# Attention in steps of two query blocks, with an order on TensorE that the scheduler may not change

## The chip, the cores and the metric

The kernel runs on one core of one Trainium2 chip. What counts is the device time of one execution of the whole program in microseconds (us). The time of the kernel before is the median of three runs.

## The reference

One layer of a hybrid decoder, for 2048 tokens of width 1024, in float32. After a projection, four mixers work on slices of its columns: stick-breaking attention (4 heads), a gating MLP over chunks, the RWKV-7 recurrence (4 heads), and forgetting attention (4 heads). Their outputs are joined and projected, and a mixture of experts follows. The change touches the two kinds of attention:

```python
HEAD_DIM, SEQ, BLOCK_Q = 64, 2048, 128
def stick_breaking_attention(q, k, v):          # 4 heads, "SB"
    for q0 in range(0, seq, BLOCK_Q):
        z = einsum('bhqd,bhkd->bhqk', q[q0:k_end], k[:k_end]) * scale
        log_one_minus = where(strict, log_sigmoid(-z), 0.0)
        between = cumsum(log_one_minus, axis=3, reverse=True) - log_one_minus
        attn = where(strict, exp(log_sigmoid(z) + between), 0.0)
        outs.append(einsum('bhqk,bhkd->bhqd', attn, v[:k_end]))
def forgetting_attention(q, k, v, log_f):       # 4 heads, "FX"
    cum = cumsum(log_f, axis=2)
    for q0 in range(0, seq, BLOCK_Q):
        logits = einsum('bhqd,bhkd->bhqk', q[q0:k_end], k[:k_end]) * scale
        logits = logits + cum[q0:k_end, None] - cum[None, :k_end]
        probs = softmax(where(causal, logits, -inf), axis=-1)
        outs.append(einsum('bhqk,bhkd->bhqd', probs, v[:k_end]))
```

Stick-breaking needs no softmax: the products of (1 - sigmoid) run along the keys from the newest to the oldest, which the kernel does with one scan per row of queries.

## The kernel before

The program is traced in this order: norm and input projection, RWKV-7 (lines 600 to 960, its products on TensorE are small), attention (from line 312), output projection (L1033 to L1106), experts. A scheduler in the compiler then orders the instructions of each engine by a simulated time line, so that RWKV-7 and attention, which do not depend on each other, lie interleaved on all engines.

Attention goes head by head, the four SB heads first and then the four FX heads. A head has 8 blocks `b` of 256 queries (two row blocks `i = 2b, 2b+1` of 128 queries, one for each half `a`), and its keys lie in chunks `c` of 512. One pass over one chunk for both halves is called a step here; a head has 20 steps. A step is made of these parts:

- logits: for each half, two float32r products (high and low part of the keys, L375 and L376) into one PSUM bank of a pool of four ("bk"), and on the diagonal a mask product (L378).
- SB: tanh on ScalarE (L390), a scale and shift on GpSimd (L391), the scan on VectorE (L393) that turns a row of 512 numbers into stick weights `S`.
- FX: VectorE adds the gates and takes the running row maximum (L402). After the last chunk of a half, two small VectorE operations make the bias (L408, L409), ScalarE takes the exponentials of all its chunks (L413), and small VectorE operations make the reciprocal of the sum (L415, L416).
- `weigh`: for each pair `p` of 128-key tiles (two pairs in a chunk), four transposes of `S` through TensorE into one bank "bk" (L425, three on the diagonal), one copy to SBUF on ScalarE (L427, tile `tq`), and two products with the values (L431; in fp32 the trace shows two records for each) into the accumulator `o`, which has one PSUM bank.
- `out`: after the last pair, VectorE and ScalarE add the halves of `o` (L442 to L457; for FX two more transposes bring the reciprocal, L455), and SP stores to `mixT`.

The transposes of one step are traced in turn with the logits of later ones by generators, half by half and pair by pair, and the scheduler may then move all of them. TensorE (PE), ScalarE (ACT), VectorE (DVE) and GpSimd (POOL) each take their instructions in the order that the scheduler wrote.

After attention the output projection reads `mixT` back in blocks of 128 tokens and multiplies it by `w_out` (L1103 to L1105).

Of the kernel before, what the change touches and what calls it, by code (L numbers as in the profile page):

```python
# [8 lines left out]
F32 = mybir.dt.float32  # L9
# [3 lines left out]
AF = mybir.ActivationFunctionType  # L13
# [294 lines left out]
def attention(tc, K, ctx, sT, sV, cumD, mixT):  # L308
# [17 lines left out]
    class Head:  # L326
# [54 lines left out]
        def spans(self, i):  # L381
            n = (i + 1) * 128
            return [(c, c * 512, min(512, n - c * 512)) for c in range(i // 4 + 1)]
# [12 lines left out]
        def softmax(self, i, S, rq):  # L396
            mx = None
            for c, x0, w in self.spans(i):
                z = self.logits(i, c, w)
                S[c] = sp.tile([128, 512], F32, name="S", tag="S")  # L400
                m = tp.tile([128, 1], F32, name="m")
                nc.vector.tensor_tensor_reduce(S[c][:, :w], z, self.nk[c][:, :w], 0.125,  # L402
                                               -3.0e38 if mx is None else mx, op0=OP.add, op1=OP.max, accum_out=m)
                mx = m
                yield
            c1 = cq[:, i, self.h:self.h + 1]
            bias = tp.tile([128, 1], F32, name="bias")
            nc.vector.tensor_add(bias, mx, c1)  # L408
            nc.vector.tensor_sub(bias, c1, bias)  # L409
            sm = tp.tile([128, 4], F32, name="sm")  # L410
            n = i // 4 + 1
            for c, x0, w in self.spans(i):
                nc.scalar.activation(S[c][:, :w], S[c][:, :w], AF.Exp, bias=bias, accum_out=sm[:, c:c + 1])  # L413
            if n > 1:
                nc.vector.tensor_reduce(sm[:, 0:1], sm[:, 0:n], AX.X, OP.add)  # L415
            nc.vector.reciprocal(rq, sm[:, 0:1])  # L416

        def weigh(self, b, p, S, o, first, last):
# [7 lines left out]
            tq = tp.tile([128, 512], F32, name="tq")  # L426
            nc.scalar.activation(tq[:, :w], t[:, :w], AF.Copy)  # L427
            for e in range(2):
# [32 lines left out]
        def block(self, b):  # L461
            S = [{}, {}]
            rq = None if self.sb else tp.tile([128, 2], F32, name="rq")
            o = []

            def weigh(p, first, last):
                if first:
                    o.append(po.tile([128, 256], F32, name="o"))
                self.weigh(b, p, S, o[0], first, last)
                if last:  # L470
                    self.out(b, o[0], rq)

            def front(c):
                if b % 2 == 0 and c == b // 2:
                    self.load(c)
                for a in range(2):
                    S[a][c] = sp.tile([128, 512], F32, name="S", tag="S")
                    self.sticks(2 * b + a, c, S[a])
                    yield

            def back(c):
                for p in range(min(2 * c + 1, b), 2 * c - 1, -1):
                    weigh(p, p == b, p == 0)
                    yield

            def front0():
                if b % 2 == 0:
                    self.load(b // 2)
                yield from self.softmax(2 * b, S[0], rq[:, 0:1])

            def mid():
                yield from self.softmax(2 * b + 1, S[1], rq[:, 1:2])

            def back0():
                for p in range(b + 1):
                    weigh(p, p == 0, p == b)
                    yield

            if self.sb:
                return [([front(c)], [], back(c)) for c in range(b // 2, -1, -1)]  # L500
            return [([front0()], [mid()], back0())]

    prev = iter(())
    for sb in (True, False):
        for h in range(NH):
            H = Head(h, sb)
            for b in range(8):
                for first, second, back in H.block(b):
                    for g in first:
                        yield from g  # L510
                    for g in second:
                        for _ in prev:
# [1363 lines left out]
```

## Time and profile before

| | |
|---|---|
| runs of the kernel before | 2602.68, 2606.71, 2612.62 us, median 2606.71 |
| profiled execution | span 2606.8 us from its first to its last instruction, at the median of the runs |
| granted TensorE clock, mean | 0.967 of full speed |
| attention on PE | 615.8 (first L375) to 1520.8 us (last product L431), SB until 1059.5 |
| RWKV-7 on PE | 534 to 1525.5 us |
| output projection on PE | from 1526.3 us |

All times are counted from the start of the span. "Busy" is the time in which an engine executes; an idle stretch of an engine is put down to what ended it, so "PE L425 <- DVE S L393" means that a transpose on PE waited for a scan on VectorE. Matmuls are pipelined in PE, so a record's duration is longer than its distance to the next record's start; it is the distance between starts that adds up. The clock of PE has two levels, 1.2 and 2.4 GHz, shown as 0.5 and 1.0, or as their mean over a stretch.

### The profile page before, as it was taken

How to read it: one execution, taken by the hardware profiler on the slowest of the kernel's cores; microseconds unless marked ns; L12 is line 12 of the kernel's file. 1: busy time of each engine (PE TensorE's matmuls, PEld its weight loads, DVE VectorE, ACT ScalarE, POOL GpSimd, SP SyncE). 2: the span in 40 equal slices, each digit the busy share in tenths (PEclk: the TensorE clock that was granted, in tenths of full speed). 3: DMA queues.
4: the chain of work that ended last, by engine and by line, in shares of the span. 5: the costliest groups of instructions: out<-in, count | busy, mean ns of one | idle time of the engine just before them, and what ended most of it. 6: DMA issues, size and time to landing. Idle time of an engine off the chain costs nothing. (4 is left out here: it accounts for less than half of the span.)

```text
span 2606.8 us, 42226 instructions
## 1 busy us (share of the span) xinstructions
PE 2442.3 (94%) x14802; PEld 1754.4 (67%) x14803; DVE 1675.3 (64%) x3881; ACT 1324.1 (51%) x2527; POOL 675.1 (26%) x691
## 2 busy tenths in 40 slices
PE   7999999997989898999999998997999999999994
PEld 6789998874656564656556667774666666676663
DVE  5313402247797869687685756665677787787885
ACT  5201222224655565675565642223667677776774
POOL 2000000015464647331332022112212232222224
PEclk9999999998989999999999999998999999999997
DMA  8510222125120211111111059443989899899995
GB/s 245 174 59 30 77 69 69 63 67 118 34 60 26 48 41 39 46 55 41 49 32 43 11 187 275 130 122 111 337 271 331 306 329 368 308 321 358 327 317 164
DMA packets 241826, 394.73 MB, mean 151 GB/s; under 512 B 65921, under 2 KB 106753, under 8 KB 241608
## 3 DMA queue, kind: packets, MB, share of 16 engines
q1 hardware_dynamic: 222472, 336.68, 39.1%
q0 software_dynamic: 19136, 55.30, 7.5%
q8 instruction: 118, 1.93, 0.3%
q14 instruction: 100, 0.82, 0.1%
HBM read 319.24 MB, written 76.85 MB: 152 GB/s over the span
## 5 line engine op out<-in xcount | busy, mean ns | idle before, releaser
L72 DVE TENSOR_TENSOR wl<-wr,wh 128x1024 fp32r<-128x1024 f32 x366 | 442.6, 1223 | 114.5 <-ACT wh L71 107.6
L71 ACT ACTIVATE wh<-wr 128x1024 fp32r<-128x1024 f32 x366 | 381.6, 1057 | 138.0 <-PE pg L1446 53.8
L393 DVE TENSOR_TENSOR_SCAN S<-S,zero 128x512 f32<-128x512 f32 (+3 forms) x160 | 197.8, 1246 | 50.5 <-POOL S L391 50.3
L152 PE MATMUL p<-hhi,wh 128*128 128x512 f32 x512 | 206.1, 404 | 14.8 <-ACT hhi L112 6.9
L425 PE MATMUL bk<-ident,S 128*128 128x128 f32 x1088 | 186.3, 292 | 24.5 <-DVE S L393 18.5
L427 ACT ACTIVATE tq<-bk 128x512 f32<-128x512 f32 (+1 forms) x288 | 156.6, 571 | 101.0 <-PE bk L425 81.4
L154 PE MATMUL p<-hhi,wl 128*128 128x512 f32 x512 | 205.2, 401 | 0.0
L153 PE MATMUL p<-hlo,wh 128*128 128x512 f32 x512 | 204.9, 400 | 0.0
L431 PE MATMUL o<-tq,v 128*64 128x256 f32 (+1 forms) x1152 | 189.3, 400 | 4.3 <-ACT tq L427 2.8
L425 PEld LDWEIGHTS bk<-ident,S 128*128 128x128 f32 x1088 | 124.0, 145 | 98.3 <-issue 53.4
L156 DVE TENSOR_TENSOR e<-p,rb 128x512 f32<-128x512 f32 x64 | 43.6, 689 | 198.3 <-PE p L154 183.9
L391 POOL TENSOR_SCALAR S<-S 128x512 f32<-128x512 f32 (+3 forms) x160 | 127.9, 808 | 145.8 <-ACT S L390 129.8
L735 POOL TENSOR_TENSOR k<-big,k 128x512 f32<-128x512 f32 x8 | 14.2, 1774 | 554.8 <-DVE big L734 548.8
L375 PE MATMUL bk<-kh,qs 128*128 128x512 f32 (+2 forms) x320 | 147.7, 462 | 7.2 <-POOL qs L351 4.8
L171 PE MATMUL p<-wh,hhi 128*128 128x256 f32 (+1 forms) x512 | 144.6, 282 | 0.0
L172 PE MATMUL p<-wl,hhi 128*128 128x256 f32 (+1 forms) x512 | 144.3, 282 | 0.0
L173 PE MATMUL p<-wh,hlo 128*128 128x256 f32 (+1 forms) x512 | 143.7, 281 | 0.0
L152 PEld LDWEIGHTS p<-hhi,wh 128*128 128x128 f32 x512 | 97.9, 191 | 40.2 <-ACT hhi L112 6.5
L413 ACT ACTIVATE S<-S,bias 128x512 f32<-128x512 f32 (+3 forms) x160 | 103.6, 649 | 34.2 <-DVE bias L409 33.7
L376 PE MATMUL bk<-kl,qs 128*128 128x512 f32 (+2 forms) x320 | 120.9, 379 | 0.0
L71 ACT ACTIVATE wh<-raw 128x512 fp32r<-128x512 f32 (+1 forms) x52 | 27.6, 589 | 179.2 <-PE p L153 171.7
L1443 PE MATMUL pg<-wh,xh 128*128 128x512 f32 x248 | 102.6, 414 | 12.6 <-ACT s L1450 12.6
(559 smaller groups left out, 6144.6 us busy)
## 6 DMA issues: line engine op xcount, KB each, us to landing
wr<-in SPq DMA_DIRECT2D x386, 512.0 KB
raw<-in SPq DMA_DIRECT2D x108, 256.0 KB
sT<-e SPq DMA_DIRECT2D x64, 256.0 KB
raw<-sT SPq DMA_DIRECT2D x128, 128.0 KB
mr<-mixT SPq DMA_DIRECT2D x16, 512.0 KB
xt<-in SPq DMA_DIRECT2D x16, 512.0 KB
xacc<-xt SPq DMA_DIRECT2D x16, 512.0 KB
h2D<-h SPq DMA_DIRECT2D x16, 512.0 KB
```

The source lines that it names most:

```text
L71: nc.scalar.activation(hi, raw, AF.Copy)
L72: nc.vector.tensor_sub(lo, raw, hi.bitcast(F32))
L152: nc.tensor.matmul(p, wh[:, k, ms], hi[j][:, k], start=(k == 0), stop=False)
L153: nc.tensor.matmul(p, wh[:, k, ms], lo[j][:, k], start=False, stop=False)
L154: nc.tensor.matmul(p, wl[:, k, ms], hi[j][:, k], start=False, stop=(k == KD - 1))
L171: nc.tensor.matmul(p, a, wh[:, k], start=first and k == 0, stop=False, skip_group_check=True)
L172: nc.tensor.matmul(p, a, wl[:, k], start=False, stop=False, skip_group_check=True)
L375: nc.tensor.matmul(z[:, :w], q, self.kh[c][:, :w], start=True, stop=False)
L393: nc.vector.tensor_tensor_scan(r, r, K.zero.to_broadcast([128, w]), 1.0 if c == i // 4 else S[c + 1][:, 0:1], op0=OP.mult, op1=OP.add)
L425: nc.tensor.transpose(t[:, x:x + 128], S[a][j // 4][:, (j % 4) * 128:(j % 4) * 128 + 128], K.ident)
L427: nc.scalar.activation(tq[:, :w], t[:, :w], AF.Copy)
L431: nc.tensor.matmul(o[64 * e:64 * e + 64, o0:256], self.v[j // 4][:, j % 4], tq[:, x0:x1], start=first, stop=last, skip_group_check=True)
```

## The change

In the new code a step is a function `front(c)` that issues the logits of both halves one after the other, and then the tanh and scan, or the maximum, of both. For FX one call of `softmax` after the last chunk serves both halves, with its small VectorE operations on two columns instead of one, and the exponentials of all chunks of both halves in a row, chunk by chunk. `back(ps)` issues the transposes of both pairs of a chunk (`turn`: up to eight, and two copies), and after them all products of both pairs (`weigh`). A `back` is issued after the `front` of a later step (`LAG = 2`, one `back` after each `front`). `tq`, `m` and `rq` have four buffers. All of it stands in `tc.manual_schedule(engines={PE})`, so that attention's instructions keep this order among themselves on PE; the scheduler still puts RWKV-7's between them, and it still orders the other engines.

```diff
-        def sticks(self, i, c, S):
-            x0 = c * 512
-            w = min(512, (i + 1) * 128 - x0)
-            z = self.logits(i, c, w)
+        def sticks(self, i, c, z, S):
+            w = z.shape[-1]
             s = S[c][:, :w]
...
-        def softmax(self, i, S, rq):
-            mx = None
-            for c, x0, w in self.spans(i):
-                z = self.logits(i, c, w)
...
-                yield
-            c1 = cq[:, i, self.h:self.h + 1]
-            bias = tp.tile([128, 1], F32, name="bias")
+        def softmax(self, b, S, mx, rq):
+            c1 = cq[:, 2 * b:2 * b + 2, self.h]
+            bias = tp.tile([128, 2], F32, name="bias")
             nc.vector.tensor_add(bias, mx, c1)
             nc.vector.tensor_sub(bias, c1, bias)
-            sm = tp.tile([128, 4], F32, name="sm")
-            n = i // 4 + 1
-            for c, x0, w in self.spans(i):
-                nc.scalar.activation(S[c][:, :w], S[c][:, :w], AF.Exp, bias=bias, accum_out=sm[:, c:c + 1])
+            sm = tp.tile([128, 2, 4], F32, name="sm")
+            n = b // 2 + 1
+            for c in range(n):
+                for a in range(2):
+                    s = S[a][c][:, 0:min(512, (2 * b + a + 1) * 128 - c * 512)]
+                    nc.scalar.activation(s, s, AF.Exp, bias=bias[:, a:a + 1], accum_out=sm[:, a, c:c + 1])
...
-        def weigh(self, b, p, S, o, first, last):
+        def turn(self, b, p, S):
             t = bank()
...
-            tq = tp.tile([128, 512], F32, name="tq")
+            tq = tp.tile([128, 512], F32, name="tq", bufs=4)
             nc.scalar.activation(tq[:, :w], t[:, :w], AF.Copy)
+            return tq
+
+        def weigh(self, b, p, tq, o, first, last):
...
+            order = [[p for p in range(min(2 * c + 1, b), 2 * c - 1, -1)] for c in chunks]
+            ends = (order[0][0], order[-1][-1])
+            def front(c):
+                if b % 2 == 0 and c == chunks[0]:
+                    self.load(top)
+                z = []
+                for a in range(2):
+                    i = 2 * b + a
+                    S[a][c] = sp.tile([128, 512], F32, name="S", tag="S")
+                    z.append(self.logits(i, c, min(512, (i + 1) * 128 - c * 512)))
+                m = None if self.sb else tp.tile([128, 2], F32, name="m", bufs=4)
+                for a in range(2):
+                    if self.sb:
+                        self.sticks(2 * b + a, c, z[a], S[a])
+                    else:
+                        self.scores(c, z[a], S[a], None if mx[0] is None else mx[0][a], m[:, a:a + 1])
+                mx[0] = None if m is None else [m[:, a:a + 1] for a in range(2)]
+                if not self.sb and c == top:
+                    self.softmax(b, S, m, rq)
+            def back(ps):
+                if ends[0] in ps:
+                    o.append(po.tile([128, 256], F32, name="o"))
+                t = [self.turn(b, p, S) for p in ps]
+                for p, tq in zip(ps, t):
+                    self.weigh(b, p, tq, o[0], p == ends[0], p == ends[1])
+                if ends[1] in ps:
+                    self.out(b, o[0], rq)
...
-    prev = iter(())
-    for sb in (True, False):
...
-                        yield from g
-                    yield from prev
-                    prev = back
-    yield from prev
+            backs = [lambda ps=ps: back(ps) for ps in order]
+            for k, c in enumerate(chunks):
+                yield (lambda: front(c)), ([backs[k]] if self.sb else backs if c == top else [])
+    LAG = 2
+    ready = []
+    n = 0
+    with tc.manual_schedule(engines={mybir.EngineType.PE}):
+        for sb in (True, False):
+            for h in range(NH):
+                H = Head(h, sb)
+                for b in range(8):
+                    for front, backs in H.block(b):
+                        front()
+                        yield
+                        ready += [(n, f) for f in backs]
+                        if ready and ready[0][0] <= n - LAG:
+                            ready.pop(0)[1]()
                             yield
-                            next(prev, None)
-                            next(g, None)
-                        yield from g
+                        n += 1
+        for _, f in ready:
+            f()
+            yield
```

How the order on the engines changes is seen at three places. The first is PE in the first SB head. L375 and L376 are logits, L425 transposes, L431 products; the other lines, here L896 to L917, are RWKV-7's. Before:

```order
L425 MATMUL bk_9957<-ident_68,S_9902 128x128
L375 MATMUL bk_9967<-kh_9564,qs_9791 128x512
L376 MATMUL bk_9967<-kl_9565,qs_9791 128x512
L896 MATMUL bk_5207<-btok_4823,wz_5193 64x64 x4
L915 MATMUL bk_5227<-wz_5193,btok_4823 64x64
L916 MATMUL bk_5227<-kv_4824 64x64
L375 MATMUL bk_9974<-kh_9564,qs_9791 128x512
L376 MATMUL bk_9974<-kl_9565,qs_9791 128x512
L913 MATMUL bk_5206<-qt_5220,M0_5204 64x128 x2
L425 MATMUL bk_9980<-ident_68,S_9934 128x128
```

The same place after, where L420 are transposes and L430 products:

```order
L430 MATMUL o_9869<-tq_9931,v_9576 64x256 x2
L896 MATMUL bk_5207<-btok_4823,wz_5193 64x64 x4
L915 MATMUL bk_5227<-wz_5193,btok_4823 64x64
L916 MATMUL bk_5227<-kv_4824 64x64
L430 MATMUL o_9869<-tq_9938,v_9576 64x256 x2
L375 MATMUL bk_9951<-kh_9566,qs_9775 128x512
L376 MATMUL bk_9951<-kl_9567,qs_9775 128x512
L375 MATMUL bk_9955<-kh_9566,qs_9775 128x512
L376 MATMUL bk_9955<-kl_9567,qs_9775 128x512
L420 MATMUL bk_9965<-ident_68,S_9878 128x128
L420 MATMUL bk_9965<-ident_68,S_9883 128x128 x2
```

The logits of the two halves stood apart, with RWKV-7's instructions and transposes between them; they now stand together, and what RWKV-7 has is put elsewhere, here between the products of a step.

The second place is PE in the last FX head, from the last logits of block 6 (`bk_15628`) to the transposes of that block's own scores (`S_15526`). After the change:

```order
L376 MATMUL bk_15628<-kl_15378,qs_15384 128x512
L378 LDWEIGHTS identb_71
L378 MATMUL bk_15628<-fx_mask_77,identb_71 128x128
...
L420 MATMUL bk_15657<-ident_68,S_15453 128x128
L430 MATMUL o_15574<-tq_15655,v_15144 64x256 x2
L430 MATMUL o_15574<-tq_15662,v_15144 64x256 x2
L420 MATMUL bk_15668<-ident_68,S_15479 128x128
L420 MATMUL bk_15668<-ident_68,S_15484 128x128 x2
L430 MATMUL o_15574<-tq_15672,v_15387 64x256
L430 MATMUL o_15574<-tq_15672,v_15387 64x128
L454 MATMUL bk_15679<-ident_68,rq_15373 128x128 x2
L420 MATMUL bk_15686<-ident_68,S_15526 128x128
```

Where "..." stands are the first seven of eight transposes. No instruction of RWKV-7 is left in this head: on PE the last of them stands ahead of it. The head has only its own products between one step's copies and the next. In the same head before, from the second half's logits of a block of the same size, the transposes of the block before stand between RWKV-7's rows:

```order
L376 MATMUL bk_15799<-kl_15633,qs_15639 128x384
L378 LDWEIGHTS identb_71
L378 MATMUL bk_15799<-fx_mask_77,identb_71 128x128
L425 MATMUL bk_15817<-ident_68,S_15650 128x128
L864 MATMUL bk_9382<-x641_4732,blk_9133 64x64 x4
L883 MATMUL bk_9389<-rhs_9016,xtf0_4716 128x128 x4
L425 MATMUL bk_15826<-ident_68,S_15650 128x128
L375 MATMUL bk_15835<-kh_15062,qs_15639 128x512
L376 MATMUL bk_15835<-kl_15063,qs_15639 128x512
L425 MATMUL bk_15817<-ident_68,S_15704 128x128
```

Each transpose, product and block of logits had others beside it that wait for other things; after, the order is step by step.

The third place is ScalarE at that same spot of the last head: L405 are the exponentials of block 6, L422 the copies behind the transposes. After the change:

```order
L422 ACTIVATE tq_15655<-bk_15650 128x512
L422 ACTIVATE tq_15662<-bk_15657 128x512
L405 ACTIVATE S_15526,sm_15638<-S_15526,bias_15635 128x512
L405 ACTIVATE S_15530,sm_15638<-S_15530,bias_15635 128x512
L405 ACTIVATE S_15563,sm_15638<-S_15563,bias_15635 128x512
L405 ACTIVATE S_15567,sm_15638<-S_15567,bias_15635 128x512
L405 ACTIVATE S_15593,sm_15638<-S_15593,bias_15635 128x512
L405 ACTIVATE S_15597,sm_15638<-S_15597,bias_15635 128x512
L405 ACTIVATE S_15622,sm_15638<-S_15622,bias_15635 128x384
L405 ACTIVATE S_15627,sm_15638<-S_15627,bias_15635 128x512
L422 ACTIVATE tq_15672<-bk_15668 128x384
```

Before (L413 exponentials, L427 copies, L866 and L885 RWKV-7's):

```order
L413 ACTIVATE S_15704,sm_15773<-S_15704,bias_15770 128x512
L413 ACTIVATE S_15728,sm_15773<-S_15728,bias_15770 128x512
L413 ACTIVATE S_15760,sm_15773<-S_15760,bias_15770 128x512
L866 ACTIVATE y6_9387<-bk_9382 64x256
L413 ACTIVATE S_15767,sm_15773<-S_15767,bias_15770 128x256
L885 ACTIVATE wz_9394<-bk_9389 128x512
L413 ACTIVATE S_15784,sm_15809<-S_15784,bias_15806 128x512
L413 ACTIVATE S_15790,sm_15809<-S_15790,bias_15806 128x512
L413 ACTIVATE S_15796,sm_15809<-S_15796,bias_15806 128x512
L413 ACTIVATE S_15803,sm_15809<-S_15803,bias_15806 128x384
L427 ACTIVATE tq_15822<-bk_15817 128x512
```

The exponentials of the two halves were two groups of four that each waited for their own bias; they are one group of eight, and the copy `tq_15672`, for which a product of the block before waits, stands behind all eight.

## Rows read from the trace of the kernel before

**Rows 1.** The page: busy time, share of the span, instructions.

```profile
PE 2442.3 (94%) x14802; PEld 1754.4 (67%) x14803; DVE 1675.3 (64%) x3881; ACT 1324.1 (51%) x2527; POOL 675.1 (26%) x691
```

**Rows 2.** Busy time by stretch: SB, FX, fourth SB head, last FX head.

```profile
core 0: us, PE busy (x) PEld busy (x) DVE busy (x) ACT busy (x) POOL busy (x), PEclk, DMA share, GB/s
615.80:1059.50 443.70, 402.74 (x2904) 253.31 (x2904) 364.92 (x598) 262.47 (x619) 255.32 (x258) 0.93 0.21 53
1059.50:1526.30 466.80, 452.15 (x3471) 286.85 (x3469) 320.58 (x1109) 288.46 (x775) 109.85 (x115) 0.99 0.15 43
953.00:1059.50 106.50, 95.31 (x705) 57.79 (x703) 98.36 (x165) 64.23 (x155) 73.93 (x72) 0.97 0.18 47
1390.70:1520.50 129.80, 128.98 (x995) 83.50 (x993) 73.44 (x268) 78.66 (x208) 11.06 (x15) 0.96 0.10 26
```

**Rows 3.** PE's waits in the SB stretch: total us, times, longest us.

```profile
PE bk L425 <- DVE S L393: 18.5, 22, 2.6
PE bk L845 <- DVE yv L839: 5.6, 6, 1.5
```

**Rows 4.** PE's waits in the FX stretch: total us, times, longest us.

```profile
PE bk L425 <- DVE m L402: 2.9, 5, 1.4
```

**Rows 5.** VectorE's waits in the SB stretch.

```profile
DVE S L393 <- POOL S L391: 50.3, 41, 4.6
```

**Rows 6.** PE's waits for copies, from 600 to 1520 us.

```profile
PE o L431 <- ACT tq L427: 2.8, 7, 0.7
PE bk L425 <- ACT tq L427: 2.1, 3, 1.4
```

**Rows 7.** PE's time line near the end: start us, duration us, instructions.

```profile
1513.32 1.08 PE L431 MATMUL o<-tq,v 128*64 128x256 f32 x8
1514.34 1.09 PE L425 MATMUL bk<-ident,S 128*128 128x128 f32 x8
1515.36 0.65 PE L431 MATMUL o<-tq,v 128*64 128x256 f32 x4
1515.94 0.66 PE L425 MATMUL bk<-ident,S 128*128 128x128 f32 x4
1516.53 0.65 PE L431 MATMUL o<-tq,v 128*64 128x256 f32 x4
```

**Rows 8.** PE's time line where logits end, at two places.

```profile
715.06 0.39 PE L376 MATMUL bk<-kl,qs 128*128 128x512 f32 x1
715.29 0.27 PE L832 MATMUL bk<-ident,xc 128*128 128x128 f32 x1
...
1418.44 0.40 PE L376 MATMUL bk<-kl,qs 128*128 128x512 f32 x1
1418.76 0.65 PE L431 MATMUL o<-tq,v 128*64 128x256 f32 x4
```

**Rows 9.** PE's time line where products wait directly behind their transposes.

```profile
723.81 0.55 PE L425 MATMUL bk<-ident,S 128*128 128x128 f32 x3 [1.73 <-DVE S L393]
725.03 0.65 PE L431 MATMUL o<-tq,v 128*64 128x256 f32 x4 [0.67 <-ACT tq L427]
```

**Rows 10.** ScalarE's time line: exponentials, then two copies.

```profile
1345.40 0.72 ACT L413 ACTIVATE S<-S,bias 128x512 f32<-128x512 f32 x1 [1.16 <-DVE bias L409]
...
1346.12 0.71 ACT L413 ACTIVATE S<-S,bias 128x512 f32<-128x512 f32 x1
...
1347.67 1.09 ACT L427 ACTIVATE tq<-bk 128x512 f32<-128x512 f32 x2 [0.26 <-PE bk L425]
```

**Rows 11.** PE's time line where attention ends and the output projection begins.

```profile
1519.32 1.51 PE L431 MATMUL o<-tq,v 128*64 128x256 f32 x12
1524.13 0.70 PE L688 MATMUL bk<-ident,big 128*128 128x128 f32 x4 [3.30 <-DVE big L684]
...
1526.28 0.77 PE L1103 MATMUL p<-wh,mh 128*128 128x512 f32 x1
...
1529.42 0.50 PE L1103 MATMUL p<-wh,mh 128*128 128x512 f32 x1 [1.17 <-DVE y L938]
```

More of the change, by code (lines that the diff above doesn't have):

```diff
@@ L394, in sticks, with scores @@
                                          1.0 if c == i // 4 else S[c + 1][:, 0:1], op0=OP.mult, op1=OP.add)
-        def softmax(self, i, S, rq):
-            mx = None
-            for c, x0, w in self.spans(i):
-                z = self.logits(i, c, w)
[L400 to L404, printed above, removed]
-                yield
-            c1 = cq[:, i, self.h:self.h + 1]
-            bias = tp.tile([128, 1], F32, name="bias")
+        def scores(self, c, z, S, mx, m):
+            w = z.shape[-1]
+            nc.vector.tensor_tensor_reduce(S[c][:, :w], z, self.nk[c][:, :w], 0.125,
+                                           -3.0e38 if mx is None else mx, op0=OP.add, op1=OP.max, accum_out=m)
+        def softmax(self, b, S, mx, rq):
+            c1 = cq[:, 2 * b:2 * b + 2, self.h]
+            bias = tp.tile([128, 2], F32, name="bias")
             nc.vector.tensor_add(bias, mx, c1)
             nc.vector.tensor_sub(bias, c1, bias)
-            sm = tp.tile([128, 4], F32, name="sm")
-            n = i // 4 + 1
-            for c, x0, w in self.spans(i):
-                nc.scalar.activation(S[c][:, :w], S[c][:, :w], AF.Exp, bias=bias, accum_out=sm[:, c:c + 1])
-            if n > 1:
-                nc.vector.tensor_reduce(sm[:, 0:1], sm[:, 0:n], AX.X, OP.add)
-            nc.vector.reciprocal(rq, sm[:, 0:1])
-        def weigh(self, b, p, S, o, first, last):
+            sm = tp.tile([128, 2, 4], F32, name="sm")
[4 more added lines that the diff above has]
+                    nc.scalar.activation(s, s, AF.Exp, bias=bias[:, a:a + 1], accum_out=sm[:, a, c:c + 1])
+            if n > 1:
+                st = tp.tile([128, 2], F32, name="st")
+                nc.vector.tensor_reduce(st, sm[:, :, 0:n], AX.X, OP.add)
+                nc.vector.reciprocal(rq, st)
+            else:
+                nc.vector.reciprocal(rq, sm[:, :, 0])
+        def turn(self, b, p, S):
             t = bank()
@@ L462, in block @@
             S = [{}, {}]
-            rq = None if self.sb else tp.tile([128, 2], F32, name="rq")
+            rq = None if self.sb else tp.tile([128, 2], F32, name="rq", bufs=4)
+            mx = [None]
             o = []
-            def weigh(p, first, last):
-                if first:
+            top = b // 2
+            chunks = range(top, -1, -1) if self.sb else range(top + 1)
+            order = [[p for p in range(min(2 * c + 1, b), 2 * c - 1, -1)] for c in chunks]
+            ends = (order[0][0], order[-1][-1])
@@ new lines, in front @@
+            def front(c):
[10 more added lines that the diff above has]
+                        self.sticks(2 * b + a, c, z[a], S[a])
+                    else:
+                        self.scores(c, z[a], S[a], None if mx[0] is None else mx[0][a], m[:, a:a + 1])
+                mx[0] = None if m is None else [m[:, a:a + 1] for a in range(2)]
+                if not self.sb and c == top:
+                    self.softmax(b, S, m, rq)
@@ L468, in weigh @@
+            def back(ps):
+                if ends[0] in ps:
                     o.append(po.tile([128, 256], F32, name="o"))
-                self.weigh(b, p, S, o[0], first, last)
-                if last:
+                t = [self.turn(b, p, S) for p in ps]
+                for p, tq in zip(ps, t):
+                    self.weigh(b, p, tq, o[0], p == ends[0], p == ends[1])
+                if ends[1] in ps:
                     self.out(b, o[0], rq)
[L473 to L497, printed above, removed]
```

14 lines of the change are left out of this document (1 added, 13 removed).

## The prediction

> **What bounds the kernel now.** I read the page first: TensorE (PE) is busy 94% of the span, VectorE 64%, ScalarE 51% [rows 1]. An average over stages says little, so I cut attention's stretch into the SB part and the FX part [rows 2]. In FX, PE is busy 452 of 467 us: the time there is PE's work and only 15 us are gaps. In SB, PE is busy 403 of 444 us, at a granted clock of 0.93 (the lower level, 1.2 GHz, for about an eighth of the stretch), and VectorE has 365 us: PE leads, VectorE is near, and in the fourth SB head it is at 98 of 106.5 us, more than PE's 95. The waits say what the gaps of PE are: in SB transposes that wait for a scan, 18.5 us in 22 pieces [rows 3], behind which VectorE itself waits 50 us for GpSimd [rows 5]; in FX almost nothing, 2.9 us for maxima [rows 4]. Waits for copies come to 2.8 + 2.1 us in all of attention [rows 6]. So there are three places for a gain: the amount of PE work, the SB scan waits, and the end of the stage; and one for a loss: the copies, hidden so far.
>
> **The change part by part.** The sum is made against the profiled span, 2606.8 us; the median of the runs is 2606.7, so nothing has to be added.
>
> *Fewer changes of kind on PE.* In the orders, attention's stretch has 1139 runs of one kind of instruction before and 822 after: 280 runs of transposes become 202, 257 of products 203, 266 of logits 168. What does a longer run save? [rows 7] give distances from start to start: eight transposes take 1515.36 - 1514.34 = 1.02 us, four 1516.53 - 1515.94 = 0.59, so one merge saves 2 x 0.59 - 1.02 = 0.16; the products of two tiles (8 records) take 1.02, of one 0.58, a merge saves 0.14. A logits product that is followed by a product with values takes 0.32, by another full-width matmul 0.23 [rows 8], so 0.09 is saved. That makes 78 x 0.16 + 54 x 0.14 + 98 x 0.09 = 12.5 + 7.6 + 8.8 = 29 us. Pricing every neighbouring pair of the two orders by the median start distance that such a pair has in the trace gives 21 to 25. I take **-25**, bounds 0 and -29.
>
> The rows show switching as a real cost, 1.16 to 1.18 us for two single runs where one long run takes 1.02 [rows 7]. The Trainium skill, TensorE: Matmul & The Clock Gate, section "Step-by-step: what each phase is for", says that the next tile's weights are loaded while the current matmul runs, pulled ahead of it, which would make a change of kind free; by that rule this term would be nothing and the sum 2626. The trace does not agree with it at these places.
>
> *Scan waits.* The distance from an SB logits product to the first transpose of the same scores, counted in PE work of the orders without any wait, has a median of 6.6 us before and 8.7 after; the shortest twentieth is below 4.4 before and below 6.8 after. Two whole steps now lie between, so most of the 18.5 us should go. What it exposes: if VectorE is late as a whole, the lag does not help. I keep 3 us of it: **-15**, bounds 0 and -18.5. FX's 2.9 us for maxima lies in the same place and is too small to count; so are the halved small VectorE operations, which nothing else on PE waits for.
>
> *Old copy waits.* The 2.8 + 2.1 us [rows 6] are replaced by the next two terms: **-5**.
>
> *Products directly behind their transposes.* Before, the products of a pair stand a median of 3.95 us of PE work behind its transposes, after only 2.0, and in 47 of 203 places a run of products directly follows the transposes. Where that occurs now, three transposes start at 723.81 and the products at 725.03 [rows 9]; the last transpose starts near 724.0, so 1.0 us passes where 0.14 would without a wait. With eight transposes the first pair's copy starts 0.5 us earlier than the last transpose and 0.36 to 0.42 us stay uncovered. Times 47, less the places where other instructions lie between: **+16**, bounds 0 (RWKV-7's rows fill all of it) and +20.
>
> *Exponentials in a burst.* An exponential of 512 takes 1346.12 - 1345.40 = 0.72 us [rows 10], so eight take some 5.6, and the copy of a pair stands behind them on ScalarE. In block 6 of the last head the third copy is behind all eight. From the last logits it takes about 1.9 us to the bias (estimate: one reduction and the small operations on VectorE), 5.6 for the exponentials, 0.5 for the copy ([rows 10]: two in 1.09) and 0.15 to the product: 8.1 us. PE has, between, eight transposes (1.02), the products of two pairs (1.02) and three transposes (0.45): 2.5 us. It waits 5.6 us. Worked the same way, blocks 2 to 7 wait 0.8, 2.3, 4.4, 2.6, 3.6 and 5.7 us, 19 together; since the copies ahead can start a little earlier I take **+17**, bounds +10 and +20. Before, this head had RWKV-7's rows beside it (busy 129.0 of 129.8 us [rows 2]) and two groups of four exponentials; after, RWKV-7 is over before the head begins. In the other three FX heads the order puts RWKV-7's rows into such places (155 of 156 times that PE goes from transposes to RWKV-7 it goes on from there to products). I take **+8** for them, bounds 0 and +48 (three heads like the last one).
>
> *One bank for `o`.* The shortest gap from the last product of a block to the first of the next falls from 2.7 to 1.45 us of PE work; VectorE's addition has to be done in it. **+3**, bounds 0 and +10.
>
> *End of the stage.* Before, RWKV-7's tail makes PE wait 3.3 us at 1524 and 1.2 us at 1529 [rows 11], while the output projection starts. After, that tail is over long before, and the loads of `w_out` are issued on SP a block ahead of attention's end. **-5**, bounds 0 and -6. Nothing on SP or GpSimd's queues is moved past something for which PE waits earlier.
>
> *The clock.* The lower level was granted where PE had gaps between small RWKV-7 products; denser SB heads could raise the 0.93, gaps in the last head lower its 0.96 [rows 2]. **0**, bounds -15 and +15.
>
> Sum: -25 - 15 - 5 + 16 + 17 + 8 + 3 - 5 = -6, so 2600.8, rounded to **2600 us**.
>
> **The rivals.** *(1) Slower, by one mechanism: the bursts of exponentials are uncovered in all FX heads.* The place is the product behind the copy behind eight exponentials. For it: ScalarE is in order, and FX left only 15 us of gaps on PE before, so nothing was idle that could be used. Against it: RWKV-7's rows stand in these places in the first three heads. It decides when RWKV-7's rows in the gaps themselves wait for VectorE or ScalarE behind the same exponentials. Full, +48 instead of +8 gives 2641; half of it 2620, which is where it begins to count as slower. Denser RWKV-7 rows in the SB part (1742 records instead of 1423) also bring VectorE's 365 us there to about 400; should it become the bound in SB, the scan term is lost and the time is about 2616. Chance 0.17.
>
> *(2) Faster: the SB part gains its idle time as well.* It has 444 - 403 = 41 us of gaps and 0.07 x 444 = 31 us lost to the clock [rows 2]. If the wide lag takes away not only the scan waits but the RWKV-7 waits beside them [rows 3], and the clock stays up, another 15 to 30 us go: 2570 to 2585. Against it: VectorE in the fourth SB head has 98 us and sets a floor. A milder form is that the copies are hidden better than I count (the +16 at 0): 2584. Chance 0.35.
>
> *(3) Changing kind costs nothing on PE*: the distances of [rows 7] then come from something else that stays, such as the reading of the results. First term 0, time 2626. The pairs speak against it. Chance 0.05.
>
> *(4) The change does not do what it says*: RWKV-7's rows split the runs again and PE does the same work with other neighbours. Then the gains and the losses both shrink, 2607. The order shows merged runs. Chance 0.05.
>
> **How the numbers follow.** My own case, 2600 with what lies within 0.5%, has 0.38. A measurement of this kernel can tell about 0.5% from no change, 13 us: below 2593.7 is faster, above 2619.7 slower. Faster 0.35 from rival 2, the same 0.38 + 0.05 = 0.43, slower 0.17 + 0.05 = 0.22. The range reaches into rivals of both signs: 2568 takes in the SB gain but not a full one with the clock, 2630 takes in half of rival 1 and all of rival 3; I leave 0.1 out at each end. The likeliest case by itself is 2594 to 2619.
>
> **What would show it.** In the profile after: PE's busy time over attention falls by some 25 us, and eight transposes or products stand in one row of the time line with about 1.02 us to the next. Transposes that wait for scans come to less than 5 us. Products that wait for copies rise from 2.8 us to 30 to 45, about 17 of it in the last FX head, as single waits of 2 to 6 us behind bursts. The gap between the last product and the steady output projection shrinks from about 8 us to 4. The forecast is wrong if PE's busy time does not fall, if waits for copies in the first three FX heads are as long as in the last, or if VectorE in the SB part is busy more than 95%.

## The result: slower by 2.4%, and the profile after

The changed kernel takes 2667.5 us (median of 4 runs, 2657.4 to 2670.4), the kernel before beside it 2608.3 (the three runs of the table with a fourth). The ratio is 1.0236, with a 95% interval of 1.0208 to 1.0263: some 60 us lost, where 2600 us was forecast. The profiled execution spans 2667.8 us.

The page shows PE with the same busy time as before [rows 1], in a longer span:

```profile
PE 2440.6 (91%) x14802; PEld 1781.9 (67%) x14803; DVE 1674.4 (63%) x3761; ACT 1319.7 (49%) x2527; POOL 660.9 (25%) x691
```

Busy time by stretch, the rows that answer to [rows 2]: the SB heads, the FX heads up to the first product of the output projection, and the last FX head:

```profile
core 0: us, PE busy (x) PEld busy (x) DVE busy (x) ACT busy (x) POOL busy (x), PEclk, DMA share, GB/s
612.85:1106.30 493.45, 431.43 (x3214) 289.04 (x3214) 396.66 (x685) 275.30 (x665) 243.13 (x262) 0.92 0.19 48
1106.30:1580.50 474.20, 419.87 (x3159) 276.63 (x3157) 290.97 (x906) 271.15 (x729) 105.98 (x140) 0.94 0.17 47
1472.70:1579.50 106.80, 83.83 (x482) 51.11 (x480) 44.82 (x151) 56.18 (x140) 6.68 (x38) 0.87 0.22 60
```

Attention's stretch grew from 910.5 to 967.7 us (57.2 of the span's 61), with 62 us of gaps in SB instead of 41 and 54 in FX instead of 15. VectorE is at 80% of the SB part, so it is not its bound as a whole. The granted clock fell from 0.93 and 0.99 to 0.92 and 0.94.

PE's waits from 612.85 to 1580.5 us (total, times, longest), for [rows 3], [rows 4] and [rows 6]:

```profile
PE o L430 <- ACT tq L422: 38.7, 47, 4.8
PE bk L832 <- DVE xc L847: 17.0, 17, 2.9
PE bk L845 <- DVE yv L839: 9.2, 8, 3.2
PE bk L688 <- DVE big L684: 6.3, 3, 3.6
PE o L430 <- DVE oo L444: 5.9, 5, 2.3
...
PE bk L420 <- DVE S L387: 1.2, 2, 0.7
```

and RWKV-7's largest in the kernel before, from 615.8 to 1526.3 us:

```profile
PE bk L845 <- DVE yv L839: 6.5, 7, 1.5
PE bk L832 <- DVE xc L847: 6.1, 8, 1.4
```

The scan waits are as good as gone, 18.5 to 1.2 us. In their place stand products that wait for copies, and RWKV-7's products (L832, L845, L688 and smaller ones) that wait for VectorE: 58.7 us in 52 pieces in all, where the kernel before had 20.2 in 27.

Where on PE do these gaps lie? I sorted each gap by attention's instruction ahead of it and behind it. Of 116 us of gaps, 26 stand directly between transposes and products; 64 stand where RWKV-7's instructions were placed between transposes and products, 46 of them in front of such an instruction and 18 in front of the product behind it; and 16 stand in front of an RWKV-7 instruction between two products of a step. Before, the first two were 2 and 4 us. PE's time line shows a place without RWKV-7, in the last head (RWKV-7's last instructions on PE are not ahead of this head, as the section on the change has it, but in its first 10 us):

```profile
1554.98 1.04 PE L420 MATMUL bk<-ident,S 128*128 128x128 f32 x8
1556.33 1.14 PE L430 MATMUL o<-tq,v 128*64 128x256 f32 x8 [0.31 <-ACT tq L422]
```

and one with RWKV-7 in the same gap, in the third SB head:

```profile
852.85 1.04 PE L420 MATMUL bk<-ident,S 128*128 128x128 f32 x8
856.79 0.33 PE L832 MATMUL bk<-ident,xc 128*128 128x128 f32 x1 [2.90 <-DVE xc L847]
857.05 0.43 PE L834 MATMUL bk<-bd,xc 128*32 128x128 f32 x8
857.40 1.08 PE L430 MATMUL o<-tq,v 128*64 128x256 f32 x8
```

In the second, 4.55 us pass from the first transpose to the first product instead of 1.35: the filler was itself late, and the products, whose copies were done at 854.6 us, stand behind it. But most such places are of another kind. At 713 us the step's copies come late as well, behind work of RWKV-7 and of the next step on ScalarE:

```profile
713.02 1.04 PE L420 MATMUL bk<-ident,S 128*128 128x128 f32 x8
...
716.55 1.03 PE L678 MATMUL bk<-bones,sq 128*128 128x2 f32 x8 [1.74 <-DVE rkT L804]
...
719.73 1.98 PE L430 MATMUL o<-tq,v 128*64 128x256 f32 x8
```

and the copies on ScalarE's time line:

```profile
718.19 1.07 ACT L422 ACTIVATE tq<-bk 128x512 f32<-128x512 f32 x2
```

Of the 46 us in front of RWKV-7's instructions only 14 lie behind the end of the step's first copy; in the rest the copy was not there yet either. In all, a step's products follow its transposes at 160 places. At 47 nothing stands between; they have 26 us of gaps, 20 of them in the last head. The other 113 are filled by RWKV-7 and have 64 us, as much for each place as the bare ones.

The bursts are as forecast. ScalarE's time line in the last head, block 6: eight exponentials, and the copy behind them, for which the longest wait of the last head stands on PE:

```profile
1560.18 0.72 ACT L405 ACTIVATE S<-S,bias 128x512 f32<-128x512 f32 x1
...
1565.00 0.71 ACT L405 ACTIVATE S<-S,bias 128x512 f32<-128x512 f32 x1
...
1565.70 0.48 ACT L422 ACTIVATE tq<-bk 128x384 f32<-128x384 f32 x1
```

and PE at the same place:

```profile
1560.93 0.55 PE L420 MATMUL bk<-ident,S 128*128 128x128 f32 x3
1566.23 1.11 PE L430 MATMUL o<-tq,v 128*64 128x256 f32 x4 [4.76 <-ACT tq L422]
```

The end of the stage on PE, for [rows 11]:

```profile
1577.91 1.20 PE L430 MATMUL o<-tq,v 128*64 128x256 f32 x8 [0.20 <-ACT tq L422]
1579.04 0.43 PE L454 MATMUL bk<-ident,rq 128*128 128x128 f32 x2
1580.54 0.96 PE L1103 MATMUL p<-wh,mh 128*128 128x512 f32 x3 [1.06 <-ACT wh L1049]
1581.83 0.50 PE L1104 MATMUL p<-wl,mh 128*128 128x512 f32 x1 [0.33 <-DVE wl L1051]
```

RWKV-7's tail no longer lies between: about 3 us from the last product to a steady projection, some 8 before.

For the balance, I cut the stretch into slices of 2 us and multiplied PE's busy time by the granted clock in each. PE's work at full clock fell from 822.5 to 789.1 us (-33); what the low level added to busy time rose from 32.4 to 62.2 (+30); the gaps rose from 55.6 to 116.4 (+61). Together +57.

### The profile page after: what moved, and what is told of

Same layout as the page of the kernel before. It is cut to its first block, busy times and chain, and to the rows that moved or that the text cites. A ratio compares the mean times of both kernels' runs of the same rounds, so it can differ in the third digit from the quotient of the medians.

```text
span 2667.8 us, 42117 instructions
## 1 busy us (share of the span) xinstructions
PE 2440.6 (91%) x14802; PEld 1781.9 (67%) x14803; DVE 1674.4 (63%) x3761; ACT 1319.7 (49%) x2527; POOL 660.9 (25%) x691
## 5 line engine op out<-in xcount | busy, mean ns | idle before, releaser
L430 PE MATMUL o<-tq,v 128*64 128x256 f32 (+1 forms) x1152 | 189.1, 414 | 45.5 <-ACT tq L422 38.7
L422 ACT ACTIVATE tq<-bk 128x512 f32<-128x512 f32 (+1 forms) x288 | 155.8, 572 | 128.6 <-PE bk L420 127.4
L420 PE MATMUL bk<-ident,S 128*128 128x128 f32 x1088 | 166.5, 289 | 1.8 <-DVE S L387 1.2
L385 POOL TENSOR_SCALAR S<-S 128x512 f32<-128x512 f32 (+3 forms) x160 | 117.4, 744 | 203.1 <-ACT S L384 185.9
L375 PE MATMUL bk<-kh,qs 128*128 128x512 f32 (+2 forms) x320 | 148.6, 465 | 4.8 <-POOL qs L351 4.8
L420 PEld LDWEIGHTS bk<-ident,S 128*128 128x128 f32 x1088 | 134.0, 150 | 24.8 <-issue 7.9
L430 PEld LDWEIGHTS o<-tq,v 128*64 128x64 f32 x1152 | 69.3, 143 | 105.5 <-ACT tq L422 69.3
L376 PE MATMUL bk<-kl,qs 128*128 128x512 f32 (+2 forms) x320 | 127.0, 397 | 0.0
L384 ACT ACTIVATE S<-bk 128x512 f32<-128x512 f32 (+3 forms) x160 | 80.4, 530 | 76.3 <-PE bk L376 53.3
```

The source lines that it names most:

```text
L375: nc.tensor.matmul(z[:, :w], q, self.kh[c][:, :w], start=True, stop=False)
L420: nc.tensor.transpose(t[:, x:x + 128], S[a][j // 4][:, (j % 4) * 128:(j % 4) * 128 + 128], K.ident)
L430: nc.tensor.matmul(o[64 * e:64 * e + 64, o0:256], self.v[j // 4][:, j % 4], tq[:, x0:x1], start=first, stop=last, skip_group_check=True)
```

## The experiments

Two theories stood at first. A: the fixed order pushes RWKV-7 forward in the schedule, so that the SB part is crowded and the last FX head bare. B: the grouped order is at fault by itself, above all the products right behind their transposes. A third, C, was added for the second group of runs: attention by itself gains, and the loss arises between it and RWKV-7. All ratios are to the kernel before on the same chip, with the 95% interval.

**Without the fixed order.**

```diff
-    with tc.manual_schedule(engines={mybir.EngineType.PE}):
+    with ExitStack():
```

> The changed kernel without the fixed order on TensorE: the same program text, but the scheduler may order attention's instructions on TensorE as it likes. Theory A (the fixed order is what costs: it pushes RWKV-7 forward in the schedule, so that VectorE holds up the stick-breaking part and nothing covers the last forgetting head): near the time before, 2590 to 2615, with waits of RWKV-7's products for VectorE back near 20 us from 59. Theory B (the grouping costs: eight exponentials in a row, products directly behind eight transposes): 2640 to 2665, with waits for copies still 25 us or more.

Measured: 2615.6 us, ratio 1.0066 (1.0046 to 1.0086). PE's waits for copies are back where they were, in this part of the list:

```profile
PE bk L832 <- DVE xc L847: 12.5, 11, 2.2
PE o L430 <- DVE oo L444: 9.1, 7, 2.3
...
PE o L430 <- ACT tq L422: 3.0, 5, 0.8
```

RWKV-7's waits for VectorE are 27.1 us. So by the ratios some 44 of the 60 us go with the fixed order, and the rewritten program without it still gains nothing: PE's work at full clock is 11 us less than before, and the gaps (+10) and the clock (+12) take that away. The waits are theory A's numbers, and the time lies at the edge of its range; the kernel before was 8 us faster on this chip (2599.9 us) than beside the change. But without the fixed order the scheduler also took the groups apart: on PE the stretch has 1159 runs of one kind before, 846 after the change and 1081 here. So the run does not part A from B, and how the fixed order costs so much it does not tell.

**Exponentials two at a time.**

```diff
-            for c in range(n):
-                for a in range(2):
...
+            def back(ps):
+                if not self.sb and len(done) <= top:
+                    exps()
```

> The changed kernel with the exponentials of a chunk (two, one for each half) issued one step ahead of that chunk's transposes, instead of all eight in a row after the last logits. Theory B: the 20.3 us of copy waits in the last forgetting head fall below 6 and the time falls by about 15 to 20, to 2648. Theory A: the copy waits fall in the same way, but that is a third of the loss only; at best 2645, and the waits of RWKV-7's products for VectorE stay at 50 us or more. Should the time not move, the copy waits were not on the path.

Measured: 2661.0 us, 1.0235 (1.0202 to 1.0267), the same as the change. The last head's waits are the same too:

```profile
PE o L434 <- ACT tq L426: 19.9, 20, 4.8
```

The experiment missed its aim: the scheduler was free on ScalarE, and as the exponentials were ready early, it put them together again in front of the copies. It tells nothing of the bursts' price.

**Products one step later.** With the rewritten exponentials, `back` becomes a generator that stops after the transposes; its products come behind the transposes of the next `back`.

```diff
                 t = [self.turn(b, p, S) for p in ps]
+                yield
...
-                            ready.pop(0)[1]()
+                            g = ready.pop(0)[1]()
+                            next(g)
+                            for _ in prev:
+                                pass
+                            prev = g
```

> The same spread exponentials, and in addition the products of a step come behind the transposes of the next step, so that a copy has a whole step of TensorE work (about 2 us) to finish. The order on TensorE stays fixed. Theory B: all 38.7 us of copy waits go but 5, time about 2630. Theory A: the copy waits go, part of what they covered comes back as waits of RWKV-7's products for VectorE (59 us to 65 or 70), time 2640 to 2650.

Measured: 2634.5 us, 1.0132 (1.0100 to 1.0165). The time does not decide: it lies nearer to theory B's 2630, but the kernel before was 8 us faster on this chip, and 1.0132 of its 2608.3 us beside the change would be 2643, inside A's 2640 to 2650. The waits speak for B: copies cost 5.2 us in all, and RWKV-7's products wait 33 us for VectorE, not the 65 or 70 of theory A. The largest of each:

```profile
PE o L434 <- ACT tq L426: 3.6, 2, 3.4
PE bk L857 <- DVE xc L872: 8.4, 10, 2.4
```

Attention is through after 863 us (the first row), where the kernel before took 905; but RWKV-7 is not, and it goes on for some 67 us with no attention left, mostly at the low clock (the second row has 60 of them):

```profile
612.70:1476.00 863.30, 798.46 (x6007) 527.45 (x6007) 650.69 (x1504) 528.28 (x1351) 358.92 (x371) 0.96 0.17 47
1480.00:1540.00 60.00, 48.62 (x333) 31.65 (x331) 23.78 (x70) 13.57 (x38) 0.00 (x0) 0.53 0.11 35
```

A new wait came too, of the first products of a block for the addition that empties the one bank of `o`:

```profile
PE o L434 <- DVE oo L448: 22.0, 12, 3.4
```

**RWKV-7 written between attention's steps.**

```diff
-            for _ in rw:
-                pass
             mix = attention(tc, K, left, sT, sV, cumD, mixT)
...
+            for s, _ in enumerate(mix):
+                while turns < (s + 1) * ROUNDS // STEPS:
+                    next(rw, None)
+                    turns += 1
```

> The changed kernel with RWKV-7 written between attention's steps in proportion (168 turns over 320 calls) instead of ahead of all of attention, so that the scheduler spreads it evenly and the last forgetting head has 155 rows of it instead of 3. Nothing else differs. Theory A: the last head's 20 us of copy waits and the low clock there go, and VectorE is less of a bound in the stick-breaking part: 2615 to 2635. Theory B: copy waits move to other heads, 2655 or more.

Measured: 2786.4 us, 1.0700 (1.0663 to 1.0736), far outside what A said. RWKV-7 now reaches into the last head, and copy waits are everywhere:

```profile
PE o L430 <- ACT tq L422: 130.4, 156, 5.5
```

This remedy of theory A failed, but the run changed more than the time at which RWKV-7 comes. Its products now stand ahead of a step's logits or of its transposes, and none of them between a step's transposes and its products, where the changed kernel has 1961 of RWKV-7's 3299 records. So all 160 places are bare, and at 143 of them the product waits for its copy, 0.78 us on the mean. What an even spread would do with them left in these places was not tried.

**Attention nearly alone, three orders.** Seven of RWKV-7's eight units are left out and zeros stand for its output, in the kernel before, in the changed kernel, and in the changed kernel with products one step later.

```diff
-            for _ in rw:
-                pass
+            y0 = init.tile([128, 512], F32, name="y0")
+            nc.vector.memset(y0, 0.0)
+            for k in range(8):
+                nc.sync.dma_start(mixT[...], y0)
```

> The kernel before with seven of RWKV-7's eight units left out (its part of the mixed output is zeros), so that attention runs nearly alone. Not compared with the kernel before but with the next run. Theory C (attention itself gains from the change, what is lost is lost between it and RWKV-7): attention's stretch on TensorE is longer here than in the next run, by 20 us or more. Theory B (the grouped order is the cost, and RWKV-7 only hides it): it is shorter here than in the next run. Theory A goes with C.

> The changed kernel with the same seven units of RWKV-7 left out. Without cover each forgetting head should wait 15 to 20 us for copies, as the last one does in the full kernel (20.3), and each stick-breaking head some 10 to 20; that is 100 to 150 us of copy waits over eight heads. Theory B: longer than the run without RWKV-7 of the kernel before. Theory C: shorter.

> The changed kernel with the products of a step behind the transposes of the next step, and with the same seven units of RWKV-7 left out. If the copies directly before their products are what attention by itself loses, copy waits fall below 20 us and the stretch is at least 80 us shorter than with the change alone. Theory C: all three differ by less than 40 us, since VectorE and ScalarE set the pace.

Measured: 2306.0 us (ratio 0.8868, 0.8834 to 0.8902), 2356.9 (0.9064, 0.9031 to 0.9097) and 2274.1 (0.8745, 0.8713 to 0.8778). The same change costs 51 us without RWKV-7, most of the 60 that it costs with it: theory C is out, and so is A as the main cause, since it needs RWKV-7 for the loss. Attention's stretch in the three kernels, first the kernel before:

```profile
612.40:1226.00 613.60, 546.89 (x3307) 317.63 (x3307) 406.11 (x860) 389.49 (x922) 280.76 (x320) 0.96 0.22 62
```

the changed kernel:

```profile
613.80:1283.80 670.00, 540.30 (x3307) 337.33 (x3307) 383.42 (x741) 387.74 (x922) 253.17 (x320) 0.91 0.20 56
```

and with late products:

```profile
612.30:1193.90 581.60, 503.17 (x3307) 333.53 (x3307) 382.09 (x740) 384.23 (x922) 277.01 (x320) 0.95 0.23 64
```

What PE waits for in the same three, before:

```profile
PE bk L425 <- DVE S L393: 23.6, 31, 1.7
PE o L431 <- ACT tq L427: 12.2, 14, 2.0
...
PE bk L425 <- DVE m L402: 10.0, 19, 1.4
```

in the changed kernel:

```profile
PE o L430 <- ACT tq L422: 119.2, 139, 4.8
```

and with late products:

```profile
PE o L430 <- DVE oo L444: 34.2, 19, 3.8
PE o L430 <- DVE oo L455: 17.8, 12, 3.3
...
PE o L430 <- ACT tq L422: 7.9, 5, 3.2
```

In the changed order 139 places wait 0.86 us each on the mean, the scan and maximum waits are gone, and PE's work at full clock falls from 525.6 to 488.4 us. One step of distance between transposes and products takes away 111 of the 119 us, and then the change is a gain of 32 us over the kernel before. That is theory B, narrowed to the copies.

**The exponentials apart, with ScalarE's order fixed too**, without RWKV-7.

```diff
-    with tc.manual_schedule(engines={mybir.EngineType.PE}):
+    with tc.manual_schedule(engines={mybir.EngineType.PE, mybir.EngineType.Activation}):
```

> The changed kernel without seven of RWKV-7's eight units (compare with the run of the change without RWKV-7), with two exponentials a step instead of up to eight in a row, and this time with ScalarE's order fixed too, since the scheduler had put the exponentials back together in the run that only rewrote them. The change without RWKV-7 has 119 us of copy waits, 55 of them in 26 places where exponentials run during the wait. If the bursts are a cost of their own, copy waits fall by 25 to 45 us and the time by as much. If only the place of the products behind their transposes counts, copy waits stay within 10 us of 119.

Measured: 2487.9 us, 0.9570 (0.9528 to 0.9611), 131 us slower than the changed kernel without RWKV-7; copy waits are 153.6 us. ScalarE's own waits show why:

```profile
ACT S L406 <- DVE bias L399: 109.5, 32, 5.9
```

The first exponentials now hold up ScalarE until their bias is there, and the copies behind them; PE also waits 51.4 us for the queries (`qs`) from GpSimd. A second miss: what the bursts cost by themselves stays open, within the 55 of the changed kernel's 119 us in which exponentials ran during a product's wait.

**The kernel before with a fixed order.**

```diff
+    with tc.manual_schedule(engines={mybir.EngineType.PE}):
         for sb in (True, False):
             for h in range(NH):
```

> The kernel before with its own order of attention fixed on TensorE and nothing else changed: products are then always directly behind their own four transposes, 288 times. If a fixed order with products behind transposes is the whole mechanism, this is much slower than both: 288 x 0.9 us = 260 us of gaps, partly filled by RWKV-7 until it is used up after five heads, so 2700 to 2800. If a fixed order by itself is harmless, below 2640.

Measured: 2995.9 us, 1.1523 (1.1472 to 1.1574), even slower than expected. The two rows are the SB heads, and the FX heads, of which three have no RWKV-7 left:

```profile
612.00:1286.90 674.90, 585.65 (x4242) 369.69 (x4242) 488.40 (x960) 335.07 (x825) 281.58 (x299) 0.88 0.15 39
1286.90:1914.70 627.80, 465.09 (x2132) 262.00 (x2130) 209.94 (x750) 224.97 (x569) 63.90 (x102) 0.65 0.11 30
```

The gaps are 252 us, near the 260 expected, but that is chance: only 140 of them are waits for copies, 0.87 us each, and 56 are transposes that wait for exponentials or scans.

```profile
PE o L431 <- ACT tq L427: 140.2, 161, 3.3
```

What the expectation lacked is the clock, 0.65 in FX, which stretches the busy time as well. So the order of the old program text was only good because it could be passed: the scheduler put an instruction of another tile ahead where a copy would run.

**Versions meant to beat both**: late products, two halves of a bank for `o`, and a lag of one step; the same with a lag of two in SB and one in FX; and the first without the fixed order.

```diff
-                    o.append(po.tile([128, 256], F32, name="o"))
+                    o.append(oo2[:, b % 2 * 256:b % 2 * 256 + 256])
...
-                        if ready and ready[0][0] <= n - LAG:
+                        if ready and ready[0][0] <= n - (LAG if sb else 1):
```

> The changed kernel with the products behind the transposes of the next step, two halves of the bank for o in turn, and a lag of one step instead of two, with RWKV-7 as it is. The order then leaves RWKV-7 only 36 rows behind the last logits (a lag of two left 91 or more, and in the run with late products RWKV-7 ran alone for 66 us at a clock of 0.5 behind attention). If balance between the two and the copy waits are what decides (theory A with its remedy): copy waits below 10 us, waits for the addition into o near 0 (25 us with late products), no stretch of RWKV-7 alone over 20 us, and 2575 to 2600, as fast as the kernel before or faster. If RWKV-7's waits for VectorE come back at 50 us or more, 2620 to 2640.

> Products behind the transposes of the next step, two halves of the bank for o, fixed order, lag two in the stick-breaking heads and one in the forgetting heads. The run with lag one everywhere had 29.9 us of waits for scans; these should fall below 8. RWKV-7 gets less room (85 rows are left behind the last logits, 36 with lag one), so it runs alone at the end for 30 to 45 us at the low clock. If that tail costs less than the scan waits did: 2590 to 2610. If it eats the gain: 2615 to 2630.

> Products behind the transposes of the next step, two halves of the bank for o, lag one, and no fixed order on TensorE: the scheduler may pass a waiting instruction by. If what the kernel before does well is only that attention's instructions can pass one another, this keeps it and adds the room: 2580 to 2600, copy waits under 6 us, scan waits under 15. If merged runs of one kind are what gains, it loses them and is at 2600 to 2615.

Measured: 2621.4 us (1.0086, 1.0056 to 1.0115), 2614.0 (1.0059, 1.0044 to 1.0074) and 2614.2 (1.0066, 1.0046 to 1.0086). None beats the kernel before. With a lag of one the scans are late again:

```profile
PE bk L422 <- DVE S L389: 29.9, 23, 5.0
```

With a lag of two in SB they are not (3.9 us), but there the additions into `o` are waited for as before, and RWKV-7 again runs on alone for 58 us, at a clock of 0.58:

```profile
PE o L432 <- DVE oo L446: 18.8, 12, 3.3
```

The stretch behind attention's end:

```profile
1477.60:1535.80 58.20, 44.11 (x306) 30.63 (x306) 22.03 (x63) 15.79 (x36) 2.17 (x1) 0.58 0.20 69
```

With a lag of one this wait is 4.3 us, none of it in SB. So it comes with the lag of two, and the two halves of `o` did not take it away as expected; why was not tried. The free order has few waits of each kind but PE's busy time of 859 us, no less than before.

## Why the prediction was wrong, by its own steps

**The copies came out right in sum, in part by luck, and their filler was counted as free.** The four terms on copies (-5, +16, +17 and +8) make +36; copy waits rose from 4.9 to 38.7 us, by 34. The bursts were sized well: in the last head five long waits make 14 us and the other sixteen 6, against +17 and half of the +16. But the other half of the +16, for the 23 bare places ahead of that head, came to 2 us, and 14 us of copy waits stand where RWKV-7's instructions lie between, 9 of them in SB, where the sum had none. That there are 47 waits and 47 bare places is chance; 26 of the waits are at bare places. The failed step is the cover: that "the order puts RWKV-7's rows into such places" was taken to mean that the gap is then paid, with +8 for three FX heads and nothing for SB. The runs show otherwise. The 113 filled places have 64 us of gaps, 0.57 us each, as much as a bare one: RWKV-7's instruction in the gap waits for VectorE itself, and in most of these gaps the step's copy is late as well. RWKV-7's waits for VectorE rose by 38 us, to 59, for which the sum had no term; in the run with products one step later they are 33. Rival 1 named the condition ("when RWKV-7's rows in the gaps themselves wait") but put it in the FX heads only, with a chance of 0.17; the SB heads, where VectorE is busiest, have 12 of the 39 us of copy waits and most of RWKV-7's.

**The clock**, the second term that failed, was put at 0, between -15 and +15. It cost +30. Time at the low level went from 71 to 133 us, in 11 stretches before and 28 after (seen in slices of 2 us). With more gaps, in nearly all the runs here, came more time at the low level: 45, 122 and 60 us in the three kernels without RWKV-7, whose gaps are 67, 130 and 78. That the gaps are the cause is argued from this order, not shown by a run of its own.

**What was right.** PE's work fell by 33 us at full clock (-25 forecast, -29 as the bound), with the same number of records in the stretch, about 6370: long runs of one kind do save. PE's busy time itself fell by 4 us only, as the low clock took the rest. So the case that changes of kind are free is refuted. What was concluded there from the Trainium skill (TensorE: Matmul & The Clock Gate, "Step-by-step: what each phase is for"), that a weight load during the running matmul makes a change of kind free, does not hold in these fp32 runs; the overlap itself was not tested. Scan waits fell by 17 us (-15). `o` cost +5 (+3). The gap at the end of the stage shrank by about 5 us (-5), though outside attention's stretch the span grew by 4.

**The rivals.** VectorE did not become the bound as a whole (397 of 493 us in SB), and RWKV-7's early end is not the main cost: 51 us are lost with most of RWKV-7 left out. Rival 2, the faster one, saw the right gain in the SB part (scan waits) and not the loss beside it. The best sum from the traces: -33 work, +30 clock, +34 copies, +38 RWKV-7 behind VectorE, -17 scans, -5 maxima, +5 `o` and some 5 of smaller waits make +57 for the stretch.

## What to carry to other kernels

A product that stands right behind its own transposes on PE waits for their copy, once for each group: 0.8 to 0.9 us on the mean in the four kernels here that have many such places. A scheduler that may put other instructions ahead hides it, a fixed order does not. Fix an order only with at least one step of other work between producer and consumer, and see that the filler does not wait for an engine that is itself late: filled places cost as much here as bare ones. And weigh the other stream: with the products one step later attention was through some 40 us sooner, but the work that had run beside it was left over at the end, and that took the gain back.

## What was not expected of the hardware

RWKV-7's small products, left alone, ran for 60 us at a granted clock of 0.53, though PE was busy for 49 of them. Attention in the bare order of the kernel before, fixed, ran at 0.65 in FX: against the kernel before its gaps grew by 196 us, and what the low level added to its busy time by 211. That the gaps brought the low level is argued here too, not shown.
